# The gate's input and the heads' norms of a three-head decoder layer, made one projection ahead

## The chip, the cores and the metric

The kernel runs on one core of a Trainium2 chip. The metric is the time of one execution in microseconds (us) on that core, smaller is better. The engines are PE (TensorE, matmuls and transposes, with its weight loads as PEld), DVE (VectorE), ACT (ScalarE), POOL (GpSimd) and SP (SyncE, which here only issues DMAs).

## What is computed

One layer of a decoder on x of 1 x 2048 x 1024 in float32: a norm, one input projection whose columns feed three groups of heads, their outputs through one output projection, then a gated MLP and a last norm. The change touches two of the groups, HGRN2 (A, 4 heads) and gated linear attention (C, 4 heads), cut here to what matters:

```python
def hgrn2_mixer(q, f_logit, i, g, lower_bound, norm_w):
    z = f_logit.astype(jnp.float32)
    f = lb + (1.0 - lb) * jax.nn.sigmoid(z)
    log_f = jnp.log(jnp.maximum(f, F_FLOOR))
    key = (1.0 - lb) * jax.nn.sigmoid(-z)
    o = chunked_gated_linear_attention(heads(q, A_DK), heads(key, A_DK), heads(i, A_DV), heads(log_f, A_DK))
    return head_rmsnorm(o, norm_w) * jax.nn.silu(g)

def gla_mixer(q, k, v, g, g_lr, w_g_up, b_g, norm_w):
    log_f = jax.nn.log_sigmoid((g_lr @ w_g_up + b_g).astype(jnp.float32)) / C_GATE_NORM
    ...
    o = chunked_gated_linear_attention(qh, kh, vh, log_f.reshape(b_sz, t, C_HEADS, C_DK))
    return head_rmsnorm(o, norm_w) * jax.nn.silu(g)
```

`head_rmsnorm` divides each head's 64 outputs of a token by the root of their mean square. `g_lr` is a projection of only 16 columns, the input of the low-rank gate.

## The kernel before

The sequence is worked in four blocks of 512 tokens (`TB`), numbered 0 to 3. For each block there are the projection steps (`in_steps`) and the mixing steps (`mix_steps`). A float32 matmul is made of three, on a high and a low part of each operand (`mm3`), so a projection to 128 columns is 24 matmuls, and each weight tile is first split by two engines into `wh` and `wl` (L106, L108, L113).

The projection steps of a block are: two for z (L252), four for V with the 16 gate columns beside it (L267), the gate (`s_gate`, L276), four for Q and K (`s_qk`, "qk projections") and four more for V. The gate transposes the 16 columns into a PSUM bank (L281), copies them to the tile `lr` (L282), multiplies by the gate's weights (L284) and works out the log decays L on ACT and DVE (L288 to L310). Its tiles come from rings: `lr` from tag X with two buffers, `e` and `u1` from tag t2 with three, the PSUM banks from tag aux with two.

The mixing steps of a block are first 14 level steps and two for the diagonal (`s_level`, `s_diag`): seven levels of 1 to 64 tokens for each half of the block. A level makes exponentials of L in a tile of tag X (L390, L393 on ACT), the scaled operands qa and kp on DVE (L394, L400) and qc on POOL (four products, L404), and score matmuls (L413, L427). Then come the windows, which apply scores and state, and the mean squares of the outputs O (`s_sq`). The norms of a block's heads (`s_out`) are left in `run["out"]` and are made within the gate of the block after next in program order, that is in the middle of `s_gate` (L303): the roots on ACT (L506, L507), their split into `hl` (L511), the spreading over the heads by 16 matmuls (L516), the product with O (L518) and a store. So block 0's norms are made at the gate of block 2 and block 1's at the gate of block 3. For the last two blocks there is no gate left; block 2's norms stand among the levels of block 3 (L704), block 3's behind its windows (L708).

`run_steps` and `merged` interleave the level steps of one block with the projection steps of the next and the scaling of x for the one after. The steps set the priorities; a scheduler then sets each engine's order, engine by engine, when the program is built. `load_w` lifts the priority of the weights' split by the numbers in `W_SPLIT`.

Of the kernel before, what the change touches and what calls it, by code (L numbers as in the profile page):

```python
# [8 lines left out]
F32 = mybir.dt.float32  # L9
# [7 lines left out]
P = 128  # L17
D = 1024
KT = D // P
TB = 512  # L20
# [24 lines left out]
def kernel(ctx: ExitStack, tc: tile.TileContext, x, norm_mix, w_in, hgrn_lower_bounds, hgrn_norm,  # L45
# [183 lines left out]
    with ExitStack() as cx:  # L229
# [13 lines left out]
        def in_steps(b, B):  # L243
# [29 lines left out]

            def s_gate():  # L276
                V, K, L = B["V"], B["K"], B["L"]
                lr = tmp.tile([16, TB], F32, name="lr", tag="X")
                pt = aux_bank()
                for t in range(NTK):  # L280
                    pe.transpose(out=pt[:16, t * P:(t + 1) * P], in_=V[:, t, 512:528], identity=ident)  # L281
                vec.tensor_copy(lr, pt[:16, :])  # L282
                gl = aux_bank()
                pe.matmul(gl, gup, lr, start=True, stop=True)  # L284
                e, u1 = t2(), t2()
                f = tmp.tile([P, 2, TB], F32, name="f", tag="f", bufs=1)
                z, l01, mn = K[:, 0:2, :], L[:, 0:2, :], L[:, 2, :]
                act.activation(e, gl, AF.Abs, bias=pc["bg"])  # L288
                act.activation(e, e, AF.Exp, scale=-1.0)
                act.activation(f, z, AF.Sigmoid)  # L290
                act.activation(z, z, AF.Sigmoid, scale=-1.0)
                vec.tensor_scalar(mn, gl, pc["bg"], 0.0, op0=ALU.add, op1=ALU.min)
                vec.tensor_scalar(u1, e, 1.0, None, op0=ALU.add)
                vec.scalar_tensor_tensor(e, u1, -1.0, e, op0=ALU.add, op1=ALU.subtract)
                for c in range(2):
                    vec.tensor_scalar(f[:, c, :], f[:, c, :], lb1[:, c:c + 1], lb[:, c:c + 1],
                                      op0=ALU.mult, op1=ALU.add)
                vec.tensor_scalar(l01, f, LN_MIN, None, op0=ALU.max)
                vec.tensor_scalar(f, f, F_FLOOR, LN_MIN, op0=ALU.max, op1=ALU.min)
                act.activation(u1, u1, AF.Ln)  # L300
                act.activation(l01, l01, AF.Ln)
                act.activation(f, f, AF.Ln, scale=LN_UP)
                if run.get("out"):  # L303
                    run.pop("out")()
                vec.tensor_tensor(e, e, u1, op=ALU.subtract)
                vec.tensor_tensor(mn, mn, e, op=ALU.add)
                vec.tensor_scalar(mn, mn, 1.0 / 16.0, None, op0=ALU.mult)
                vec.scalar_tensor_tensor(l01, f, lnc, l01, op0=ALU.subtract, op1=ALU.add)
                for c in range(2):
                    vec.tensor_scalar(K[:, c, :], K[:, c, :], lb1[:, c:c + 1], None, op0=ALU.mult)  # L310
            for t in range(NTK):
                steps.append(lambda t=t: (s_vw(C_V, 272) if t == 0 and b > 0 else None, s_v(272, 256, t)))
            steps.append(s_gate)


            def s_qk(nm, c, col, scale):
                if nm not in B:
# [2 lines left out]
            for nm, c, col, scale in (("Q", 0, A_Q, 1.0), ("Q", 1, A_Q + P, 1.0), ("Q", 2, C_Q, C_SCALE),  # L320
                                      ("K", 2, C_K, 1.0)):
                steps.append(lambda a=(nm, c, col, scale): s_qk(*a))
            for t in range(NTK):
                steps.append(lambda t=t: (s_vw(A_I, 256) if t == 0 else None, s_v(256, 0, t)))

# [21 lines left out]
        def mix_steps(b, B):  # L347
# [153 lines left out]
                    pe.matmul(ms[32 * c:32 * c + 32, :HT], hcol[:, 0:32], sq[:, c, :], start=True, stop=True)  # L501
                copy(vec, B["ms"][:, sl], ms[:, :HT])

            def s_out():
                O, ms = B["O"], B["ms"]
                act.activation(ms, ms, AF.Ln, bias=eps_t, scale=1.0 / 64.0)  # L506
                act.activation(ms, ms, AF.Exp, scale=-0.5)  # L507
                for hb in range(NH):
                    sl = slice(hb * HT, (hb + 1) * HT)
                    hl = tmp.tile([P, 2, HT], F32R, name="hl", tag="t2", bufs=3)  # L510
                    split(ms[:, sl], hl[:, 0, :], hl[:, 1, :])  # L511
                    for g2 in range(2):
                        r = aux_bank().rearrange("p (c t) -> p c t", c=2)
                        for c in range(2):
                            for i in range(2):
                                pe.matmul(r[:, c, :], sel[:, 2 * g2 + c, :], hl[:, i, :], start=(i == 0), stop=(i == 1))  # L516
                        cs = slice(2 * g2, 2 * g2 + 2)
                        vec.tensor_tensor(O[:, cs, sl], O[:, cs, sl], r, op=ALU.mult)  # L518
# [6 lines left out]
            for hb in range(NH):  # L525
                steps2.append(lambda hb=hb: s_decay(hb))
                steps2 += [lambda hb=hb, w=w: s_window(hb, w) for w in range(NW)]
                steps2.append(lambda hb=hb: s_sq(hb))
            steps2.append(lambda: run.update(out=s_out))
            return steps, steps2  # L530


# [158 lines left out]
            blocks[b]["hT"] = norms[b].hT  # L691
            return steps

        ins = ins[0:2] + ins[3:5] + ins[2:3] + ins[5:]
        run_steps(ins, prep(1), 0.5, 0.7)
        for b in range(NB):
            lv, wn = mix_steps(b, blocks[b])
# [3 lines left out]
                lv = lv[3:]  # L701
            if b == NB - 1:
                lv_prio = tc.cur_priority
                mid = [run.pop("out")] if NB > 1 else []  # L704
                run_steps(lv, bg + mid, 0.0, 0.6)
                ac_prio = tc.cur_priority
                run_steps(wn)
                run.pop("out")()  # L708
            else:
                ins, late, bg = in_steps(b + 1, blocks[b + 1])  # L710
                run_steps(lv, merged(ins, prep(b + 2)), 0.0, 0.6)
# [603 lines left out]
```

## Time and profile before

| | us |
|---|---|
| median of 3 runs | 2220.92 |
| lowest and highest | 2212.77, 2224.83 |
| the profiled execution | 2215.95 |
| its span on the core | 2214.2 |
| PE busy in the span | 2142.7 (97%) |
| DVE busy | 1678.8 (76%) |
| ACT busy | 987.5 (45%) |
| POOL busy | 349.3 (16%) |

The profile is of one execution. Its page gives each engine's busy time, and the trace behind it can be asked for stretches of the span, for what an engine waited for and what ended the wait, and for the instructions of an engine in order of time. Matmuls are pipelined and their ends are modelled, so a matmul of 512 columns is shown longer than the distance to the next one. The mixer of the A and C groups, in which the changed code lies, takes about the first 640 us of the span; behind it come the B group, the output projection and the MLP, whose code is the same before and after.

### The profile page before, as it was taken

What the parts mean: (1) busy time and instruction counts of PE and PEld (TensorE: products, weight loads), DVE (VectorE), ACT (ScalarE), POOL (GpSimd) and SP (SyncE); (2) the same over time, 40 slices, a digit from 0 to 9 for tenths busy, and PEclk for the clock granted to TensorE, in tenths of its full rate; (3) what the DMA queues carried; (4) which work ended last, traced back from release to release, by engine and by line L of the source; (5) the groups of instructions that cost most, each with busy time, mean ns of one, the idle gap of its engine ahead of it and who ended that gap; (6) DMA issues with size and microseconds to landing.
All of it is one profiled execution on the core that took longest, in us unless ns stands there. A gap on an engine that the chain in (4) does not pass through costs nothing.

```text
span 2214.2 us, 31440 instructions
## 1 busy us (share of the span) xinstructions
PE 2142.7 (97%) x12118; PEld 1761.8 (80%) x12118; DVE 1678.8 (76%) x2366; ACT 987.5 (45%) x1361; POOL 349.3 (16%) x456
## 2 busy tenths in 40 slices
PE   7999999999899999999999999999999999999998
PEld 6887778777667878988888887788888887888886
DVE  7799998988768778786676766666666678679676
ACT  3453535433156467454444445544444455226332
POOL 2232341516333231000000000000000000000000
PEclk9999999999999999999999999999999999999999
DMA  7352432345144736643342435522222258667653
GB/s 260 116 180 73 162 97 65 96 148 184 60 136 176 225 121 190 202 136 119 110 134 87 133 95 182 190 80 86 86 86 86 85 176 276 209 205 254 217 174 111
DMA packets 313699, 321.41 MB, mean 145 GB/s; under 512 B 17347, under 2 KB 267214, under 8 KB 312014
## 3 DMA queue, kind: packets, MB, share of 16 engines
q1 hardware_dynamic: 313550, 319.41, 44.5%
q8 instruction: 95, 1.56, 0.3%
q14 instruction: 54, 0.44, 0.1%
HBM read 233.38 MB, written 85.98 MB: 144 GB/s over the span
## 4 chain that ended last, share of the span: by engine, by line
PE 54%; DVE 7%; DMA 5%; ACT 2%; issue 2%; POOL 0%; SPq 0%; DVEq 0%; POOLq 0%; ACTq 0%
PE mm L1072 26%; PE sc L1072 13%; PE aux L1072 6%; PE sc L137 2%; PE sc L138 2%; PE sc L136 2%; DVE wl L113 1%; DMA x_d<-xr 1%; PE mm L138 1%; PE mm L136 1%; PE mm L137 1%; DMA xt<-x_d 1%; DVE xc L801 1%; DMA y<-ps_d 1%; PE mm L913 1%
## 5 line engine op out<-in xcount | busy, mean ns | idle before, releaser
L106 ACT ACTIVATE wh<-wr 128x1024 fp32r<-128x1024 f32 (+3 forms) x217 | 200.8, 928 | 354.6 <-PE mm L1072 91.2
L113 DVE TENSOR_TENSOR wl<-wr,wh 128x1024 fp32r<-128x1024 f32 (+2 forms) x241 | 260.8, 1085 | 102.5 <-ACT wh L106 98.3
L106 ACT ACTIVATE wh<-s 128x1024 fp32r<-128x1024 f32 x116 | 123.0, 1062 | 251.7 <-PE sc L1072 197.8
L138 PE MATMUL mm<-hTh,wl 128*128 128x512 f32 x576 | 231.0, 401 | 2.8 <-POOL wl L113 2.4
L136 PE MATMUL mm<-hTh,wh 128*128 128x512 f32 x576 | 233.6, 406 | 0.0
L137 PE MATMUL mm<-hTl,wh 128*128 128x512 f32 x576 | 231.7, 402 | 0.0
L404 POOL TENSOR_TENSOR qc<-Q,X 32x128 f32<-32x128 f32 x224 | 151.0, 674 | 247.3 <-ACT X L390 116.4
L1072 PE MATMUL mm<-t34h,wh 128*128 128x512 f32 x464 | 181.1, 390 | 1.3 <-DVE y L1238 0.9
L1072 PE MATMUL mm<-t34h,wl 128*128 128x512 f32 x464 | 180.6, 389 | 0.0
L1072 PE MATMUL mm<-t34l,wh 128*128 128x512 f32 x464 | 180.5, 389 | 0.0
L113 DVE TENSOR_TENSOR wl<-s,wh 128x1024 fp32r<-128x1024 f32 x116 | 141.4, 1221 | 18.5 <-ACT wh L106 18.4
L137 PE MATMUL sc<-wl,oh 128*128 128x256 f32 x512 | 146.8, 287 | 2.4 <-DVE wl L113 2.4
L136 PE MATMUL sc<-wh,oh 128*128 128x256 f32 x512 | 146.3, 287 | 0.2 <-DVE xr L834 0.2
L138 PE MATMUL sc<-wh,ol 128*128 128x256 f32 x512 | 145.4, 284 | 0.0
L138 PEld LDWEIGHTS mm<-hTh,wl 128*128 128x128 f32 x576 | 108.6, 189 | 31.1 <-issue 4.3
L136 PEld LDWEIGHTS mm<-hTh,wh 128*128 128x128 f32 x576 | 108.4, 188 | 28.9 <-issue 6.8
L137 PEld LDWEIGHTS mm<-hTl,wh 128*128 128x128 f32 x576 | 108.7, 189 | 27.8 <-issue 7.3
L1141 DVE SCALAR_TENSOR_TENSOR ga<-gr,pcol,ga 128x1024 f32<-128x1024 f32 x84 | 107.6, 1281 | 0.4 <-issue 0.3
L1072 PEld LDWEIGHTS mm<-t34h,wh 128*128 128x128 f32 x464 | 87.1, 188 | 21.2 <-issue 1.7
L137 PEld LDWEIGHTS sc<-wl,oh 128*128 128x128 f32 x512 | 97.5, 190 | 5.8 <-DVE wl L113 3.0
L1072 PEld LDWEIGHTS mm<-t34h,wl 128*128 128x128 f32 x464 | 87.1, 188 | 18.2
L1072 PEld LDWEIGHTS mm<-t34l,wh 128*128 128x128 f32 x464 | 87.1, 188 | 17.9
(335 smaller groups left out, 5508.4 us busy)
## 6 DMA issues: line engine op xcount, KB each, us to landing
wr<-in_w_in_dram SPq DMA_DIRECT2D x80, 512.0 KB
wr<-in_ffn_w_gate_dram SPq DMA_DIRECT2D x42, 512.0 KB
wr<-in_ffn_w_val_dram SPq DMA_DIRECT2D x42, 512.0 KB
wr<-in_w_out_dram SPq DMA_DIRECT2D x32, 512.0 KB
gr_d<-v SPq DMA_DIRECT2D x32, 512.0 KB
ps_d<-y SPq DMA_DIRECT2D x32, 512.0 KB
wr<-gr_d SPq DMA_DIRECT2D x32, 512.0 KB
wr<-in_ffn_w_down_dram SPq DMA_DIRECT2D x25, 512.0 KB
```

Source lines behind the costliest of these rows:

```text
L106: act.activation(o, i, AF.Copy)
L113: e_lo.tensor_tensor(lo, raw, hi.bitcast(F32), op=ALU.subtract)
L136: pe.matmul(o, lh, rh, start=first, stop=False)
L137: pe.matmul(o, lh, rl, start=False, stop=False)
L138: pe.matmul(o, ll, rh, start=False, stop=last)
L404: pool.tensor_tensor(qc[p_, h, :].rearrange("p (n s) -> p n s", s=lev), qo[p_, 2], xo[p_, 2], op=ALU.mult)
L801: vec.tensor_tensor_scan(xc[:, i, :], r[:, i, :], th[:, i, :], initial=hs0[:, c:c + 1], op0=ALU.mult, op1=ALU.add)
L913: pe.transpose(out=pt[:, k * P:(k + 1) * P], in_=xt[:, (k0 + k) * P:(k0 + k + 1) * P], identity=ident)
L1072: pe.matmul(o, lhs[a], rhs[b], start=first and k == 0 and i == 0, stop=last and k == KH - 1 and i == 2, skip_group_check=True)
L1141: vec.scalar_tensor_tensor(ga, gr[:, k:k + TH], pc[f"fw{k}"][:, f:f + 1], ga, op0=ALU.mult, op1=ALU.add)
```

## The change

The gate is cut in two steps. `s_gate_in` transposes and copies `lr` and calls the first part of the norms, if there are any; `s_gate` multiplies, calls the second part of the norms at once (before its own work on ACT and DVE), and goes on as before. In the list of steps `s_gate_in` stands behind the first qk projection and `s_gate` behind the second; before, the whole gate stood ahead of the first one (in block 0 behind the second, by a line that is now gone). `s_out` is cut in the same way: `s_out_in` makes the roots and both `hl`, `s_out` the matmuls, the products and the store. Where block 2's norms stand among the levels, the two parts are now two steps; at the end they follow each other.

```diff
--- before.py
+++ after.py
@@ -273,15 +273,21 @@
 
 
 
-            def s_gate():
-                V, K, L = B["V"], B["K"], B["L"]
-                lr = tmp.tile([16, TB], F32, name="lr", tag="X")
+            def s_gate_in():
+                lr = B["lr"] = tmp.tile([16, TB], F32, name="lr", tag="X")
                 pt = aux_bank()
                 for t in range(NTK):
-                    pe.transpose(out=pt[:16, t * P:(t + 1) * P], in_=V[:, t, 512:528], identity=ident)
+                    pe.transpose(out=pt[:16, t * P:(t + 1) * P], in_=B["V"][:, t, 512:528], identity=ident)
                 vec.tensor_copy(lr, pt[:16, :])
+                if run.get("out"):
+                    run["out"][0]()
+
+            def s_gate():
+                K, L = B["K"], B["L"]
                 gl = aux_bank()
-                pe.matmul(gl, gup, lr, start=True, stop=True)
+                pe.matmul(gl, gup, B["lr"], start=True, stop=True)
+                if run.get("out"):
+                    run.pop("out")[1]()
                 e, u1 = t2(), t2()
                 f = tmp.tile([P, 2, TB], F32, name="f", tag="f", bufs=1)
                 z, l01, mn = K[:, 0:2, :], L[:, 0:2, :], L[:, 2, :]
@@ -300,8 +306,6 @@
                 act.activation(u1, u1, AF.Ln)
                 act.activation(l01, l01, AF.Ln)
                 act.activation(f, f, AF.Ln, scale=LN_UP)
-                if run.get("out"):
-                    run.pop("out")()
                 vec.tensor_tensor(e, e, u1, op=ALU.subtract)
                 vec.tensor_tensor(mn, mn, e, op=ALU.add)
                 vec.tensor_scalar(mn, mn, 1.0 / 16.0, None, op0=ALU.mult)
@@ -310,8 +314,6 @@
                     vec.tensor_scalar(K[:, c, :], K[:, c, :], lb1[:, c:c + 1], None, op0=ALU.mult)
             for t in range(NTK):
                 steps.append(lambda t=t: (s_vw(C_V, 272) if t == 0 and b > 0 else None, s_v(272, 256, t)))
-            steps.append(s_gate)
-
 
             def s_qk(nm, c, col, scale):
                 if nm not in B:
@@ -320,6 +322,9 @@
             for nm, c, col, scale in (("Q", 0, A_Q, 1.0), ("Q", 1, A_Q + P, 1.0), ("Q", 2, C_Q, C_SCALE),
                                       ("K", 2, C_K, 1.0)):
                 steps.append(lambda a=(nm, c, col, scale): s_qk(*a))
+
+            steps.insert(NTK + 3, s_gate_in)
+            steps.insert(NTK + 5, s_gate)
             for t in range(NTK):
                 steps.append(lambda t=t: (s_vw(A_I, 256) if t == 0 else None, s_v(256, 0, t)))
 
@@ -501,14 +506,21 @@
                     pe.matmul(ms[32 * c:32 * c + 32, :HT], hcol[:, 0:32], sq[:, c, :], start=True, stop=True)
                 copy(vec, B["ms"][:, sl], ms[:, :HT])
 
-            def s_out():
-                O, ms = B["O"], B["ms"]
+            def s_out_in():
+                ms = B["ms"]
                 act.activation(ms, ms, AF.Ln, bias=eps_t, scale=1.0 / 64.0)
                 act.activation(ms, ms, AF.Exp, scale=-0.5)
+                B["hl"] = []
+                for hb in range(NH):
+                    hl = tmp.tile([P, 2, HT], F32R, name="hl", tag="t2", bufs=3)
+                    split(ms[:, hb * HT:(hb + 1) * HT], hl[:, 0, :], hl[:, 1, :])
+                    B["hl"].append(hl)
+
+            def s_out():
+                O = B["O"]
                 for hb in range(NH):
                     sl = slice(hb * HT, (hb + 1) * HT)
-                    hl = tmp.tile([P, 2, HT], F32R, name="hl", tag="t2", bufs=3)
-                    split(ms[:, sl], hl[:, 0, :], hl[:, 1, :])
+                    hl = B["hl"][hb]
                     for g2 in range(2):
                         r = aux_bank().rearrange("p (c t) -> p c t", c=2)
                         for c in range(2):
@@ -526,7 +538,7 @@
                 steps2.append(lambda hb=hb: s_decay(hb))
                 steps2 += [lambda hb=hb, w=w: s_window(hb, w) for w in range(NW)]
                 steps2.append(lambda hb=hb: s_sq(hb))
-            steps2.append(lambda: run.update(out=s_out))
+            steps2.append(lambda: run.update(out=(s_out_in, s_out)))
             return steps, steps2
 
 
@@ -691,7 +703,6 @@
             blocks[b]["hT"] = norms[b].hT
             return steps
 
-        ins = ins[0:2] + ins[3:5] + ins[2:3] + ins[5:]
         run_steps(ins, prep(1), 0.5, 0.7)
         for b in range(NB):
             lv, wn = mix_steps(b, blocks[b])
@@ -701,11 +712,12 @@
                 lv = lv[3:]
             if b == NB - 1:
                 lv_prio = tc.cur_priority
-                mid = [run.pop("out")] if NB > 1 else []
+                mid = list(run.pop("out")) if NB > 1 else []
                 run_steps(lv, bg + mid, 0.0, 0.6)
                 ac_prio = tc.cur_priority
                 run_steps(wn)
-                run.pop("out")()
+                for f in run.pop("out"):
+                    f()
             else:
                 ins, late, bg = in_steps(b + 1, blocks[b + 1])
                 run_steps(lv, merged(ins, prep(b + 2)), 0.0, 0.6)
```

PE, around the gate of block 2 (at about 260 us). The rows in a row before; `mm` is a projection, `aux<-ident,V` the transposes for the gate, `aux<-lr,gup` the gate's matmul:

```order
L281 MATMUL aux<-ident,V 16x128 x4
L136 MATMUL mm<-hTh,wh 128x512
L137 MATMUL mm<-hTl,wh 128x512
L138 MATMUL mm<-hTh,wl 128x512
L136 MATMUL mm<-hTh,wh 128x512
L137 MATMUL mm<-hTl,wh 128x512
L138 MATMUL mm<-hTh,wl 128x512
L136 MATMUL mm<-hTh,wh 128x512
L137 MATMUL mm<-hTl,wh 128x512
L138 MATMUL mm<-hTh,wl 128x512
L136 MATMUL mm<-hTh,wh 128x512
L284 MATMUL aux<-lr,gup 128x512
```

And now, at the end of the second qk projection, where the gate's matmul and the norms' matmuls (`aux<-hl,sel`) come:

```order
L137 MATMUL mm<-hTl,wh 128x512
L138 MATMUL mm<-hTh,wl 128x512
L288 MATMUL aux<-lr,gup 128x512
L528 MATMUL aux<-hl,sel 128x256 x4
L432 MATMUL sc<-qa_549,kp_547 64x64 x4
L432 MATMUL sc<-qc_551,kp_547 64x128 x2
L432 MATMUL sc<-qa_549,kp_547 64x64 x4
L432 MATMUL sc<-qc_551,kp_547 64x128 x2
L136 MATMUL mm<-hTh,wh 128x512
L137 MATMUL mm<-hTl,wh 128x512
L528 MATMUL aux<-hl,sel 128x256 x4
```

The transposes have moved a projection ahead of the gate's matmul, the gate's matmul a projection and a half later, and the norms' matmuls, which stood within the first two projections, stand directly behind it, with a level's score matmuls (`sc`) next.

DVE, around the gate of block 3 (at about 390 us), before: the subtraction that makes the low part of `hl` stands within the gate's work (L292, L293, L294):

```order
L108 CAST wh<-wr 128x1024
L292 TENSOR_SCALAR L<-aux,pcol_412 128x512
L293 TENSOR_SCALAR t_4083<-t_4082 128x512
L400 TENSOR_TENSOR qa_550<-Q,X 64x2x128
L294 SCALAR_TENSOR_TENSOR t_4082<-t_4083,t_4082 128x512
L113 TENSOR_TENSOR hl<-ms,hl 128x256
L113 TENSOR_TENSOR wl<-wr,wh 128x1024
L518 TENSOR_TENSOR O<-O,aux 128x2x256 x2
L113 TENSOR_TENSOR hl<-ms,hl 128x256
```

And now, at the start of block 3's projections, where K is copied from the z projections:

```order
L361 TENSOR_TENSOR pr<-Q,K 128x768
L377 COPY_PREDICATED sd_543<-mdiag,dsb 128x1024
L113 TENSOR_TENSOR hl<-ms,hl 128x256
L108 COPY K<-mm 128x512
L113 TENSOR_TENSOR wl<-wr,wh 128x816
L113 TENSOR_TENSOR hl<-ms,hl 128x256
L108 COPY K<-mm 128x512
L108 COPY dT<-aux 96x256
L113 TENSOR_TENSOR wl<-wr,wh 128x544
```

Both subtractions have moved ahead by some 30 instructions, to the copies of K from the two z projections.

ACT, around the gate of block 2, before; X is a level's tile, L290 and L291 are the sigmoids and L301 and L302 the logarithms of the gate:

```order
L290 ACT_TABLE_LOAD
L290 ACTIVATE f<-K 128x1024
L291 ACTIVATE K<-K 128x1024
L301 ACT_TABLE_LOAD
L301 ACTIVATE L<-L 128x1024
L302 ACTIVATE f<-f 128x1024
L390 ACT_TABLE_LOAD
L390 ACTIVATE X<-L 128x192x2
L393 ACTIVATE X<-X 128x192x2
```

And now:

```order
L395 ACTIVATE X<-L 128x384
L395 ACTIVATE X<-L 128x192x2
L297 ACT_TABLE_LOAD
L297 ACTIVATE K<-K 128x1024
L398 ACT_TABLE_LOAD
L398 ACTIVATE X<-X 128x192x2
L307 ACT_TABLE_LOAD
L307 ACTIVATE L<-L 128x1024
L308 ACTIVATE f<-f 128x1024
L321 ACTIVATE Q<-mm 128x512
L395 ACT_TABLE_LOAD
L395 ACTIVATE X<-L 128x192x2
```

The two sigmoids no longer stand together, so that exponentials come between them with a table load each way (two more loads stand just ahead of these rows), and the last exponential of X here comes behind the copy of Q out of the first qk projection.

## Rows read from the trace of the kernel before

**Rows 1.** Stretches: from:to, length, busy PE, PEld, DVE, ACT, POOL, clock, DMA, GB/s
```profile
246.00:321.00 75.00, 69.14 (x614) 57.55 (x615) 72.25 (x118) 35.56 (x54) 34.73 (x51) 1.00 0.29 85
321.00:376.00 55.00, 54.78 (x469) 42.84 (x469) 47.11 (x88) 21.06 (x34) 2.97 (x4) 1.00 0.28 78
376.00:449.00 73.00, 69.02 (x602) 57.09 (x603) 69.55 (x115) 35.21 (x52) 35.42 (x52) 1.00 0.25 74
...
540.00:571.00 31.00, 23.94 (x195) 18.27 (x192) 30.59 (x45) 5.32 (x11) 18.91 (x27) 1.00 0.57 203
```

**Rows 2.** PE's waits, 120 to 571 us: releaser, us in total, times, longest
```profile
PE sc L427 <- DVE qa L400: 9.4, 8, 2.8
PE sc L413 <- DVE qa L400: 4.1, 5, 1.9
PE aux L516 <- DVE hl L113: 2.2, 3, 1.2
...
PE aux L281 <- DVE V L108: 1.3, 2, 1.1
...
PE aux L284 <- DVE lr L282: 0.4, 2, 0.3
PE aux L516 <- DVE O L518: 0.4, 1, 0.4
```

**Rows 3.** PE in order of time: start, us, instruction, idle before and releaser
```profile
269.99 0.97 PE L516 MATMUL aux<-hl,sel 128*128 128x256 f32 x6 [0.73 <-DVE hl L113]
...
274.68 0.39 PE L136 MATMUL mm<-hTh,wh 128*128 128x512 f32 x1
274.91 0.39 PE L137 MATMUL mm<-hTl,wh 128*128 128x512 f32 x1
...
541.34 0.98 PE L516 MATMUL aux<-hl,sel 128*128 128x256 f32 x6 [1.17 <-DVE hl L113]
...
558.72 0.42 PE L427 MATMUL sc<-qa,kp 128*32 128x64 f32 x8 [2.79 <-DVE qa L400]
```

**Rows 4.** DVE in order of time, pauses and the subtractions of hl
```profile
247.44 0.44 DVE L108 COPY V<-mm 128x272 f32<-128x272 f32 x1 [0.51 <-PE mm L138]
...
257.10 0.69 DVE L108 CAST wh<-wr 128x1024 fp32r<-128x1024 f32 x1 [0.37 <-PE mm L138]
...
371.34 0.69 DVE L108 COPY K<-mm 128x512 f32<-128x512 f32 x1 [2.69 <-PE mm L138]
...
397.57 0.68 DVE L113 TENSOR_TENSOR hl<-ms,hl 128x256 fp32r<-128x256 f32 x1
...
400.50 0.41 DVE L113 TENSOR_TENSOR hl<-ms,hl 128x256 fp32r<-128x256 f32 x1
```

**Rows 5.** ACT in order of time, around the gate at 260 us
```profile
245.53 1.28 ACT L290 ACT_TABLE_LOAD   x1
246.82 1.06 ACT L290 ACTIVATE f<-K 128x1024 f32<-128x1024 f32 x1
...
265.19 0.52 ACT L390 ACTIVATE X<-L 128x384 f32<-128x384 f32 x1
...
272.62 0.58 ACT L319 ACTIVATE Q<-mm 128x512 f32<-128x512 f32 x1
```

**Rows 6.** POOL in order of time, the four products of one level
```profile
256.73 3.82 POOL L404 TENSOR_TENSOR qc<-Q,X 32x128 f32<-32x128 f32 x4 [5.28 <-ACT X L390]
```

**Rows 7.** DVE in order of time, lr and the level behind it
```profile
260.45 1.21 DVE L113 TENSOR_TENSOR wl<-wr,wh 128x1024 fp32r<-128x1024 f32 x1
...
262.68 0.71 DVE L282 COPY lr<-aux 16x512 f32<-16x512 f32 x1
263.32 0.53 DVE L392 TENSOR_TENSOR X<-L 128x384 f32<-128x384 f32 x1
263.78 0.54 DVE L397 TENSOR_TENSOR L<-L 128x384 f32<-128x384 f32 x1
264.25 0.41 DVE L400 TENSOR_TENSOR qa<-Q,X 64x256 f32<-64x256 f32 x1
```

## The prediction

> **What bounds the kernel now.** The page's table of engines comes first: PE is busy 97% of the span, so little can be won outside its waits, and the question is whether the waits that the edit aims at set the end. I read three views for that, in this order. The first gives each engine's busy time by stretches of the mixer stage [rows 1]. The reader is to see two kinds of stretch taking turns. From 246 to 321 us, where block 2's projections run beside the levels of block 1, DVE works 72.25 of 75 us and PE 69.14; the same pair for block 3 (376 to 449 us) has DVE at 69.55 of 73; the levels of the last block (540 to 571 us) have DVE at 30.59 of 31 and PE at 23.94. Between them, in the windows from 321 to 376 us, PE works 54.78 of 55 and DVE has slack. So around both gates that also hold the norms, DVE is the bound and PE is the engine that waits; DVE's idle time there, 2.75 + 3.45 + 0.41 = 6.6 us, is all that a better order can take out of these stretches without taking work out of DVE.
>
> The second view is what PE waited for between 120 and 571 us [rows 2]. The three kinds of matmul that the edit touches wait 1.3 us (transposes for V, two waits), 0.4 us (the gate's matmul for lr, two) and 2.2 + 0.4 us (the norms' matmuls for hl and for O, four): 4.3 us in eight waits. The levels' score matmuls wait far more, 9.4 + 4.1 us, and always for DVE. The third is PE's order of time [rows 3]: the norms' matmuls stand 0.73 us at 269.99 and 1.17 us at 541.34, but after the last of these the levels' matmuls wait 2.79 us at 558.72 before the same stretch is over. A PE that is let go earlier at the first place waits longer at the second, as long as DVE's work ends when it ended.
>
> **The change part by part.** *No work is added but table loads.* The same matmuls, copies and subtractions are issued.
>
> *The waits of transposes, gate and norms.* They sum to 4.3 us of idle time [rows 2]. The idle time is counted from the modelled end of the matmul before, 0.39 us after its start, while the next one could have started 0.23 us after it [rows 3], so each of the eight hides up to 0.16 us more: 4.3 + 8 x 0.16 = 5.6 us at most. In the new order the norms' matmuls stand directly behind the gate's and their hl is made a whole projection ahead, so these PE waits go. What is late next is DVE's queue in the same stretch: the score matmuls of the last levels. I therefore count 0 of the 5.6 in the sum and keep 5.6 for the range.
>
> *The subtractions that make hl.* In the block with the gate at 376 to 449 us they took 0.68 + 0.41 us inside the stretch in which DVE is the bound. Now they stand between the copies of the two z projections, where DVE idled 2.69 us for PE at 371.34 [rows 4]. That is work leaving the bound engine's stretch: -1.1 us. For the block before it, with its gate at 246 to 321 us, I take nothing: the same move puts hl there ahead of work of DVE's own, so it is done earlier and not beside a wait.
>
> *Two pauses of DVE on the projections.* At 247.44 and 257.10 DVE waited 0.51 and 0.37 us for PE [rows 4]. With one level step less among the first V tiles PE gets there earlier, so they go: -0.9 us.
>
> *The gate's place.* For blocks 1 to 3 its rest moves behind the second of the qk projections, and with it the levels shift against the projections. The piece of ACT's order shows what this brings: the exp of the next level's X now stands behind the copy of Q out of the first projection and behind a table load, where it stood ahead of them. From the end of that projection to that exp's end it is 0.58 (copy of Q) + 1.28 (load) + 0.52 (exp) = 2.4 us [rows 5], and POOL's four products then take 3.82 us [rows 6]: the scores can start 6.2 us after the projection's end. PE reaches them after 13 matmuls of 0.23 = 3.0 us, so a new PE wait of about 3 us stands in the next projection, once at each of the two gates. What it costs is read on DVE. After the projection's end DVE has the cast of the next weights (0.69, [rows 4]), lr (0.71) and the subtraction (0.53) = 1.9 us before it needs the exp at 2.4: 0.5 idle. Then sum (0.54), two qa (0.41 each), kp (of the sum's shape, 0.54 too) and the weights' low part (1.21) [rows 7] bring it to 5.5; the next level's X has to wait till 6.2, because lr holds one of the two X buffers and POOL reads the other: 0.7 idle; and the copy of the scores waits for PE after that, about 0.4. Together 1.6 us, less about half a microsecond by which I take DVE to come late to that point anyway, with its queue full: +1.1 us at each of two gates, +2.2. Bounds: 0 if DVE is later by 1.6 than I take it, and +5.8 if the whole PE wait of 2 x 2.9 is lost.
>
> *Table loads.* ACT's order has three more of them in the block at 246 us, none more elsewhere: 3 x 1.28 = 3.8 us of ACT [rows 5], which is busy 35.56 of 75 us there [rows 1]. I count 0; the cover is ACT's idle half, and if it is gone, they cost up to 3.8. By the Trainium skill (ScalarE: Activation LUTs, What ACT_TABLE_LOAD costs) a switch of table costs a drain of about 1.38 us beside the load, 2.66 us in all; the rows speak against that here, since the next activation starts 1.29 us after the load began (245.53 and 246.82), and by that page the three would take 8.0 us of ACT and the exp behind each gate would come 1.4 us later.
>
> *The DMA queue.* The store of O moves behind three more weight loads on SP. What it stores is read only after the mixer stage, and O is next written in the windows behind the levels; 0.
>
> *The two places without a projection between.* In the last block the norms' input and matmuls are a level step apart, and at the end of the stage nothing lies between them; PE's order at the end is the old one, so the waits there stay. 0.
>
> The sum: -1.1 - 0.9 + 2.2 = +0.2 us against the profiled execution's 2215.95, 2216.2. The median of the runs shown is 4.97 us above that execution, so the forecast is 2221 us.
>
> **The rivals.** *The gain is kept.* If DVE's queue runs dry less often because PE delivers projections earlier, all of PE's eight waits go and stay gone: -5.6 - 1.1 - 0.9 = -7.6 us, some 2213 us by the median. For it: these waits lie on PE, which is busy 97%. Against it: DVE at 72.25 of 75, and score waits of 13.5 us that can take all of it back [rows 1, 2]. Only more than this, half of those score waits too, would be faster by over 0.5%.
>
> *The wait changes its place and grows (slower).* lr now lives across a projection in a ring of two X buffers. Each level's exps then wait for POOL's four products of the level before, for two levels in a row at each gate; the second costs what POOL is late against DVE's queue, up to one more 3.82 less its own 13 matmuls, about 1 us, and the whole PE wait of 5.8 counts, with the three table loads in front of exps: 5.8 + 2 x 1 + 3.8 - 1.1 = +10.5 us, 2231 us. The point from which it decides: POOL's products against 3.1 us of DVE work that stands behind the exp [rows 6, 7]; at 3.82 POOL is past it by 0.7. For it: the order puts exp behind the copy of Q at both gates. Against it: DVE's own backlog, which makes the same instructions late without any wait.
>
> *It doesn't do what it says.* The scheduler could have put hl and lr where they were. The order shows hl ahead by some 30 DVE instructions at two of its four places and hardly moved at the other two, so this holds in part, and is in the sum.
>
> **How the numbers follow.** Forecast (the waits are traded, +0.2, between -3 and +4): 0.55. Gain kept (-7.6): 0.2. Slower rival (+10.5): 0.25. The measurement tells about 0.5%, 11 us, from no change. The runs of one kernel lie 12 us apart, so a median can be off by 3 or 4: of the gain's 0.2 about 0.1 ends beyond -11, of the slower rival's 0.25 about 0.12 beyond +11, and I add 0.02 on either side for orders that I have not followed. So faster 0.12, same 0.74, slower 0.14. The range reaches to both rivals and leaves out what lies beyond them: 2210 to 2232.
>
> **What would show each step.** Right: the matmuls of gate and norms wait for nothing at the gates of blocks 2 and 3; hl's subtractions stand before 375 us at 0.41 each; the score matmuls inside the second qk projection wait some 3 us for POOL or DVE; DVE stays near 72 of 75. The gain kept would show in the levels' score waits, still 13.5 us or less, and the stretches from 246 and 376 us shorter by 2 to 3 us each. The slower rival would show as DVE idle for POOL in front of the X subtraction, over 1.5 us at each gate. The forecast is wrong if the stretch up to 246 us, or the one before 120 us, in which only the order of projections and x loads changes, moves by more than a microsecond, since I gave both nothing.

## The result, and the profile after

The changed kernel is slower: 2234.59 us median (2229.68 to 2245.16, 8 runs) against 2220.07 for the kernel before (8 runs), a ratio of 1.0079 with a 95% interval of 1.006 to 1.0098, 14.5 us. A second set of runs gave 1.0075 (1.0052 to 1.0098). The prediction said 2221 us, between 2210 and 2232, and gave "slower by over 0.5%" a chance of 0.14: it was wrong.

The profiled execution took 2240.93 us, 25.0 more than that of before. The loss is read first where the levels of blocks 0, 1 and 2 run, beside which the gates of blocks 1, 2 and 3 stand. Each line goes from a block's first diagonal step to its last level-32 score matmul; the columns are those of [rows 1]. The first fence is the kernel before, the second the changed one, blocks 0 to 3 in both:

```profile
72.50:184.80 112.30, 109.43 (x844) 92.28 (x843) 94.80 (x151) 47.44 (x74) 36.56 (x56) 1.00 0.45 142
212.20:314.80 102.60, 96.00 (x855) 79.23 (x853) 95.81 (x161) 49.01 (x78) 39.17 (x54) 1.00 0.43 145
346.60:443.20 96.60, 92.82 (x839) 76.74 (x837) 87.25 (x150) 48.61 (x72) 36.00 (x52) 1.00 0.28 80
477.10:559.60 82.50, 77.67 (x626) 59.70 (x625) 72.37 (x107) 28.89 (x51) 44.41 (x56) 1.00 0.61 205
sum 394.00, PE 375.93 PEld 307.96 DVE 350.23 ACT 173.95 POOL 156.15; mean PE 93.98 PEld 76.99 DVE 87.56 ACT 43.49 POOL 39.04
```

```profile
75.80:193.70 117.90, 110.18 (x827) 92.86 (x827) 96.25 (x153) 47.61 (x75) 38.76 (x56) 0.98 0.43 135
222.60:329.70 107.10, 98.16 (x854) 81.55 (x854) 94.51 (x162) 53.34 (x81) 34.52 (x55) 0.98 0.41 139
361.40:461.00 99.60, 93.31 (x838) 77.59 (x836) 87.12 (x150) 48.27 (x72) 32.56 (x52) 0.98 0.27 77
494.90:577.30 82.40, 77.37 (x626) 59.69 (x624) 72.38 (x106) 28.89 (x51) 44.43 (x56) 1.00 0.61 205
sum 407.00, PE 379.02 PEld 311.68 DVE 350.25 ACT 178.12 POOL 150.27; mean PE 94.75 PEld 77.92 DVE 87.56 ACT 44.53 POOL 37.57
```

DVE's work is the same to 0.02 us (350.23 and 350.25), and the stages are 13.0 us longer: all of that is new idle time of DVE, 4.15 us beside the gate of block 1, 5.80 beside that of block 2, 3.13 beside that of block 3, nothing in the block without a gate. The mean clock of the three stages fell from 1.00 to 0.98, so a part of this idle time may be DVE waiting for a slower PE. Of the other 12 us of the profiled difference 5.6 lie between 605 and 656 us, where the clock is lower (below), and some 3.3 ahead of the first stage; of these 1.46 are left at 107 us. Read between the same matmuls (106.43, 183.94, 312.47 and 442.30 us before; 107.89, 192.24, 326.88 and 460.12 us now), the stretches of the three gates take 6.8, 6.1 and 3.4 us longer.

What PE waited for from 120 to 590 us in the changed kernel, the view of [rows 2]:

```profile
PE sc L432 <- DVE qa L405: 15.8, 11, 3.2
PE sc L432 <- POOL qc L409: 3.4, 3, 1.3
PE mm L136 <- DVE wh L108: 2.6, 2, 1.4
PE sc L418 <- DVE qa L405: 2.1, 2, 1.7
...
PE aux L528 <- DVE hl L113: 1.5, 1, 1.5
```

The transposes and the gate's matmul wait no more, the norms' matmuls only once (in the last block). But the score matmuls wait 15.8 + 2.1 us for DVE where they waited 13.5, and 3.4 us for POOL, where it was 0.2.

The place where it begins, at the gate of block 2: ACT, POOL, DVE and PE of the changed kernel in order of time, as in [rows 5], [rows 6], [rows 7] and [rows 3].

```profile
276.38 0.60 ACT L321 ACTIVATE Q<-mm 128x512 f32<-128x512 f32 x1 [8.70 <-PE mm L138]
277.00 1.28 ACT L395 ACT_TABLE_LOAD   x1
278.29 0.56 ACT L395 ACTIVATE X<-L 128x384 f32<-128x384 f32 x1
```

```profile
257.59 5.73 POOL L409 TENSOR_TENSOR qc<-Q,X 32x128 f32<-32x128 f32 x8 [1.12 <-ACT X L395]
...
278.93 4.12 POOL L409 TENSOR_TENSOR qc<-Q,X 32x128 f32<-32x128 f32 x4 [15.61 <-ACT X L395]
```

```profile
278.88 0.56 DVE L402 TENSOR_TENSOR L<-L 128x384 f32<-128x384 f32 x1 [0.97 <-ACT X L395]
...
283.08 0.56 DVE L397 TENSOR_TENSOR X<-L 128x384 f32<-128x384 f32 x1 [0.41 <-POOL qc L409]
284.21 1.30 DVE L441 COPY_PREDICATED sd<-mask,sc 128x512 f32<-128x512 int32 x1 [0.58 <-PE sc L432]
```

```profile
281.36 0.45 PE L432 MATMUL sc<-qa,kp 128*64 128x64 f32 x8 [1.72 <-DVE qa L405]
283.10 0.44 PE L432 MATMUL sc<-qc,kp 128*64 128x128 f32 x4 [1.28 <-POOL qc L409]
```

ACT stands idle for 8.70 us in front of the copy of Q, because its instructions run in their order and that copy needs the projection's end; the next level's exponential is queued behind the copy and a table load. POOL had finished the level before at 263.3 and stands idle 15.61 us. When the exponential is through, DVE, POOL and PE wait in turn. The same waits come at the gate of block 3 (PE 1.71 and 1.28 at 415 and 417 us) and smaller ones at that of block 1 (PE 0.36 and 0.82 at 153 and 155, DVE 1.40 us for POOL at 155).

### The profile page after: what moved, and what is told of

It reads as the page before. It is cut to its first block, busy times and chain, and to the rows that moved or that the text cites. A ratio compares the mean times of both kernels' runs of the same rounds, so it can differ in the third digit from the quotient of the medians.

```text
span 2239.2 us, 31437 instructions
## 1 busy us (share of the span) xinstructions
PE 2155.9 (96%) x12118; PEld 1772.6 (79%) x12118; DVE 1677.6 (75%) x2366; ACT 992.8 (44%) x1364; POOL 347.4 (16%) x456
## 4 chain that ended last, share of the span: by engine, by line
PE 53%; DVE 6%; DMA 5%; ACT 3%; issue 2%; POOL 0%; SPq 0%; DVEq 0%; POOLq 0%; ACTq 0%
PE mm L1084 26%; PE sc L1084 13%; PE aux L1084 6%; DMA x_d<-xr 1%; PE sc L137 1%; PE sc L138 1%; PE sc L136 1%; DMA xt<-x_d 1%; DVE wl L113 1%; DMA y<-ps_d 1%; PE mm L136 1%; PE mm L138 1%; PE mm L137 1%; DVE xc L813 1%; PE mm L925 1%
## 5 line engine op out<-in xcount | busy, mean ns | idle before, releaser
L409 POOL TENSOR_TENSOR qc<-Q,X 32x128 f32<-32x128 f32 x224 | 144.4, 645 | 279.7 <-ACT X L395 175.7
```

Source lines behind the costliest of these rows:

```text
L409: pool.tensor_tensor(qc[p_, h, :].rearrange("p (n s) -> p n s", s=lev), qo[p_, 2], xo[p_, 2], op=ALU.mult)
```

## The experiments

Ratios are to runs of the kernel before on the same chip, with their 95% intervals. The edits are cut to what matters (`...`); they are against the changed kernel, or, where the text says so, against the kernel before.

**The two halves of the change.** The gate alone (cut and moved; the norms whole, as before):

```diff
-                if run.get("out"):
-                    run["out"][0]()
...
-                if run.get("out"):
-                    run.pop("out")[1]()
...
+                if run.get("out"):
+                    run.pop("out")()
```

> The gate is split and moved as in the changed kernel; the norms stay whole, in the middle of the gate. Theory of the order (the next level's exp stands behind the copy of Q on ACT, so POOL's products and then the scores come late, PE waits, and the clock falls after such waits): slower as the changed kernel, 2228 to 2237 us, with score waits of 1 to 2 us for DVE and 1 us for POOL inside the second qk projection at three gates. Theory of the norms (two hl held over a projection take two of three t2 buffers): no slower than before, 2216 to 2224 us.

Measured: 2233.04 us, ratio 1.0078 (1.0047 to 1.0108), with the waits of the changed kernel (1.70 and 1.28 us at 277 and 279 us, 2.94 at 191 us), as the theory of the order expected.

The norms alone (the gate whole at its old place, the norms' first part one V projection ahead):

```diff
+            if b > 1:
+                steps.insert(len(steps) - 1, s_norm_in)
             steps.append(s_gate)
```

> The gate is whole and at its old place; only the norms are in two parts, the first one V projection ahead of the gate. Theory of the order: the exp stands ahead of the copy of Q as before, so 2216 to 2225 us, clock 0.993 or more. Theory of the norms: 2228 us or more.

Measured: 2221.58 us, 1.0022 (1.0004 to 1.004), in the expected range; the mean clock, 0.992 over its runs, is a little below the 0.993 expected. So nearly all of the loss comes with the gate.

**Another place for the same cut.** Both parts of the gate one projection earlier, the input right behind V:

```diff
-            steps.insert(NTK + 3, s_gate_in)
-            steps.insert(NTK + 5, s_gate)
+            steps.insert(NTK + 2, s_gate_in)
+            steps.insert(NTK + 4, s_gate)
```

> Both parts of the change, but the gate's input directly behind V and its matmul behind the first qk projection, so the input is one projection ahead and nothing of the gate is more than one projection later. Theory of the order: ACT has the level's exp ahead of the first copy of Q again, so 2214 to 2224 us. If being split, not the order on ACT, is what costs: 2228 us or more.

Measured: 2223.75 us, 1.0021 (1.0006 to 1.0035), at the end of the expected range, and no score matmul waits for POOL. Here too lr is written one projection before its matmul. So being one projection ahead is not by itself what costs; this place is.

The kernel before with its gate whole, moved behind the second qk projection:

```diff
-            steps.append(s_gate)
...
+            steps.insert(NTK + 4, s_gate)
...
-        ins = ins[0:2] + ins[3:5] + ins[2:3] + ins[5:]
```

> The kernel before with its whole gate moved behind the second qk projection in every block; lr is used at once and no buffer is held over a projection. Theory of the order: the exp stands behind two copies of Q, so slower, 2228 to 2240 us. Theory that lr's hold on one of two X buffers is what costs: 2216 to 2224 us.

Measured: 2229.07 us, 1.0055 (1.0033 to 1.0077), with score waits of 1.60, 1.28 and 2.46 us at 164, 172 and 193 us. The later place is slow for a whole gate too, in which lr is used at once and holds no buffer over a projection.

**Which gate.** The changed kernel with block 1's gate at its old place, and the mirror, blocks 2 and 3 at the old place:

```diff
-            steps.insert(NTK + 3, s_gate_in)
-            steps.insert(NTK + 5, s_gate)
+            steps.insert(NTK + (2 if b == 1 else 3), s_gate_in)
+            steps.insert(NTK + (3 if b == 1 else 5), s_gate)
```

> The changed kernel, but block 1's gate (the one beside the levels of block 0, 130 to 200 us) has both parts at the old place, right behind the projections of V; the gates of blocks 2 and 3 and the norms stay as changed. Theory of three gates: the offset of the changed kernel against the kernel before grew from 1.5 to 8.3 us between 107 and 192 us, so this run gets some 5 to 7 us back: 2227 to 2230 us. Rival, the prediction's own count (block 1's gate costs nothing, all is at blocks 2 and 3): 2233 to 2236 us.

> The mirror of the run with block 1's gate at the old place: here block 1's gate (and block 0's, which has no levels beside it) has the new place, and the gates of blocks 2 and 3 have both parts right behind V. Theory of three gates: the norms-only run was 1.0022 times the kernel before, and block 1's gate adds 5 to 7 us: 2226 to 2230 us, with PE's waits of 0.8 us or more at 154 and near 3 us at 190 us and none for POOL behind 200 us. Rival, the prediction's count (block 1 costs nothing): 2220 to 2223 us.

Measured: 2230.56 us, 1.0047 (1.0031 to 1.0063), and 2230.80 us, 1.0054 (1.0035 to 1.0073). Both times lie within 1 us above the range of the theory of three gates; the mirror has the waits expected (0.82 us at 152, 2.92 at 189, none for POOL behind 200), and beside them new ones of 2.50 and 2.51 us at 283 and 415. Block 1's gate costs about 0.3% either way (0.79 - 0.47, and 0.54 - 0.22 of the norms alone), some 7 us, as many as the 6.8 read between the same matmuls above. The other two together cost about 0.25%, by differences whose intervals are about 0.2% wide on either side: three gates, where the prediction had counted two.

**The held buffer.** In the changed kernel lr is written one projection before its matmul, and takes one of two X buffers for so long. Here it takes one of t2's three instead, and in the second run a part of L that the gate itself writes just behind that matmul, which costs no buffer of any ring:

```diff
-                lr = B["lr"] = tmp.tile([16, TB], F32, name="lr", tag="X")
+                lr = B["lr"] = tmp.tile([16, TB], F32, name="lr", tag="t2", bufs=3)
```

```diff
-                lr = B["lr"] = tmp.tile([16, TB], F32, name="lr", tag="X")
+                lr = B["lr"] = B["L"][:16, 2, :]
```

> The changed kernel with one thing else: the gate's input lr (16 partitions) takes a buffer of the ring t2 and not one of the two buffers X that the levels' exponentials write. The order of ScalarE then has the exponentials of the next level ahead of the copy of Q at the gates of blocks 2 and 3 again, at the price of six more table loads in the program. Theory of the order (the next level's exponential stands behind the copy of Q and a table load because its buffer X is held): PE's waits at the scores of these two gates, 1.72 + 1.28 and 1.71 + 1.28 us in the changed kernel, fall under 1 us each, and the time falls from 2235 to some 2222 to 2229 us. Rival, the place (the gate's VectorE work now falls on other levels, whatever buffer lr has): the waits stay or go to the next level, and the time stays at 2231 to 2238 us.

> The changed kernel, but lr stands in 16 partitions of the third part of L, which the gate itself writes right behind its matmul: no buffer X and none of t2. Theory of the held buffer (lr, written one projection before its matmul, holds one of the two X buffers and keeps the next level's exponential behind the copy of Q): at least the 6 us at equal clock that lr in t2 gave back are given back, without the cost of t2's ring: 2218 to 2225 us, no wait of the scores for POOL and none near 3 us at the level-32 scores of block 0. Rival, the place (the gate behind the second projection of Q costs whatever buffer lr has, as with the whole gate there, which stayed at 2241 us with lr in t2): 2226 to 2234 us.

Measured: 2223.62 us, 1.0035 (1.0012 to 1.0057), and 2225.74 us, 1.0022 (1.0006 to 1.0037). The second run's stages, and ACT at the gate of block 2:

```profile
74.30:188.30 114.00, 109.57 (x829) 92.13 (x828) 95.11 (x151) 50.13 (x76) 39.99 (x56) 0.99 0.45 140
215.70:319.20 103.50, 97.42 (x855) 80.86 (x853) 94.50 (x161) 55.94 (x83) 36.56 (x54) 0.98 0.44 143
351.10:449.00 97.90, 93.52 (x839) 77.68 (x837) 87.26 (x150) 51.17 (x74) 31.61 (x52) 0.98 0.27 79
```

```profile
266.75 0.52 ACT L395 ACTIVATE X<-L 128x384 f32<-128x384 f32 x1
...
271.39 0.58 ACT L321 ACTIVATE Q<-mm 128x512 f32<-128x512 f32 x1
```

The exponential now stands ahead of the copy of Q, the waits for POOL and the 2.94 us at block 0's level-32 scores are gone, and the three stages take 9.2 us less than in the changed kernel (324.6 became 315.4; before 311.5). So its data can be ready before the copy's; in the changed kernel it stood behind the copy, and ACT idle. The first run is in the range of its theory; the second is between those of theory and rival. ACT's order has nine table loads more than before here, three more in the changed kernel: the number of loads does not decide the time.

Is the buffer all of it? The same gate with lr in L, but the norms whole, beside the changed kernel on one chip:

> The gate cut in two and moved as in the changed kernel, the norms whole as before, and lr in the third part of L. Theory that the shares add up (norms' split 0.22%, gate's move 0.57%, all of the latter from lr in the ring X): no difference from the kernel before, ratio 0.998 to 1.003, 2215 to 2226 us. Rival (the place itself costs beside the buffer, and the norms' split then happens to cost nothing in the run with lr in L): ratio 1.003 to 1.006, 2226 to 2233 us.

> The changed kernel once more, on the same chip and beside the same runs of before as the run of the gate alone with lr in L. Expected: ratio 1.006 to 1.010 again, 2230 to 2240 us. The theory of the held buffer says the other run of this call lies at least 8 us under it; the rival says at most 5.

Measured: 2227.80 us, 1.0043 (1.0028 to 1.0057), against 2236.80 us, 1.0075. The two differ by 9 us, in the buffer and also in the norms, which are cut in the second alone. Since the gate alone with lr in X lost as much as the whole change (1.0078), the 9 us are put down to the buffer; the like pairs of runs give it 0.35% (gate alone, 1.0078 and 1.0043) and 0.44 or 0.57% (whole change, 1.0079 and 1.0035 or 1.0022). With 0.43% left the shares do not add up, and the rival holds for the rest: the place costs beside the buffer. One row of it is a level-32 score wait of 3.91 us at 321.56 us.

**lr out of the ring elsewhere.** The kernel before with lr in t2 and in L, the gate one projection earlier with both, the whole gate at the later place with both (the line that makes lr is edited as above; the place as in the runs above):

> The kernel before, with lr alone moved from the ring X to the ring t2. Theory of the ring: at the old place too lr takes one of the two X buffers, but gives it back at once, so there is little to gain: 2214 to 2219 us against 2218 to 2219 for the kernel before. Rival (the ring of t2, which the gate's own e and u1 and the norms' hl use, becomes the narrow place, and the exponentials that come earlier bring more table loads): 2220 to 2226 us.

> The kernel before with lr in the third part of L. Theory of the held buffer: before gives X back at once, so only little is held: 2214 to 2219 us. Rival (the exponentials that then run ahead of the gate's logarithms push the gate itself back on ScalarE, which is what cost 5.6 us at equal clock with lr in t2, not t2's ring): 2220 to 2226 us.

> The run with both parts of the gate one projection earlier (gate's input right behind V, gate behind the first projection of Q; 2223.75 us), with lr in the ring t2. Theory of the ring: the exponentials run ahead of the copies of Q at all gates and the 2 us that run kept over the kernel before at equal clock go: 2214 to 2220 us, and if any version of this change beats the kernel before it is this one. Rival (what is left is the norms' split and more table loads): 2221 to 2226 us.

> The run with both parts one projection earlier (2223.75 us; 2228.04 with lr in t2), with lr in the third part of L. Theory of the held buffer: 2215 to 2221 us, the best of all versions. Rival (exponentials ahead of the gate's logarithms push the gate back, PE waits for V's copy as with lr in t2): 2223 to 2229 us.

> The kernel before with its gate whole and moved behind the second projection of Q, as in the place-only run (2229 us), but lr in a buffer of the ring t2 and not in one of the two X. Theory of the ring (what the gate costs at its later place is that lr takes a turn of the two X buffers, so that the next level's exponentials stand behind the copies of Q): 2219 to 2224 us, and PE's waits of the place-only run at 164 and 172 us (1.60 and 1.28) and for POOL at 425 us (0.85) go or fall under half. Rival, the place alone (the gate's work collides with other levels whatever lr's buffer is): 2227 to 2231 us with waits of the same size.

> The kernel before with the whole gate behind the second projection of Q (2229 us; 2241 with lr in t2), and lr in the third part of L. Theory that t2's ring made the 6 us wait for lr's copy at 418 us: 2218 to 2226 us. Rival, the place: 2227 to 2236 us.

Measured, in this order: 1.0008 (0.9985 to 1.003), 1.0014 (0.9997 to 1.003), 1.0038 (1.0022 to 1.0053), 1.0041 (1.0024 to 1.0057), 1.009 (1.0064 to 1.0116), 1.0062 (1.0042 to 1.0083); in us 2222.29, 2220.52, 2228.04, 2227.65, 2241.59 and 2235.53. The theory missed all six: four times lie in the rival's range, and two (2228.04 and 2241.59) above both. Nowhere but with the cut gate at the changed kernel's place does a free X buffer help. The two homes of lr agree within their intervals, so nothing shows that t2's ring is what harms. With the whole gate the wait only moves, here from the run with lr in L:

```profile
417.93 2.04 PE L284 MATMUL aux<-L,gup 16*128 16x512 f32 x2 [5.99 <-DVE L L282]
```

PE stands 6 us because the copy of lr comes late in DVE's order. "lr in the ring is the cause" is therefore shown for the changed kernel alone, and there for a part of its loss. No version was measured faster than the kernel before.

## The granted clock behind the new waits

In its profiled execution the kernel before is at full clock (2.4 GHz) from 0 to 640 us. The changed kernel drops to the lower level (1.2 GHz) for a few microseconds behind most of its longer waits; a stretch in which the column after POOL's is below 1.00 holds such a drop. First the line of before and that of the changed kernel:

```profile
0.00:640.00 640.00, 602.47 (x4656) 476.14 (x4657) 542.82 (x944) 252.98 (x391) 204.79 (x287) 1.00 0.41 130
```

```profile
0.00:640.00 640.00, 595.67 (x4556) 474.24 (x4557) 527.86 (x921) 246.09 (x380) 191.33 (x281) 0.97 0.39 125
```

Then three drops of the changed kernel, first from its first profile, then from its second one, in which the same instructions stand 1 to 3 us earlier:

```profile
192.00:200.00 8.00, 7.76 (x44) 5.26 (x45) 5.56 (x11) 2.05 (x4) 1.79 (x4) 0.60 0.00 0
280.00:292.00 12.00, 9.35 (x71) 6.70 (x72) 9.36 (x14) 4.94 (x9) 5.86 (x10) 0.86 0.18 50
608.00:622.00 14.00, 14.00 (x47) 8.52 (x45) 2.56 (x4) 1.34 (x2) 2.72 (x2) 0.51 0.14 37
```

```profile
190.00:200.00 10.00, 9.10 (x56) 6.55 (x57) 8.74 (x16) 3.11 (x5) 1.80 (x4) 0.83 0.04 11
279.00:291.00 12.00, 10.72 (x74) 7.79 (x70) 7.83 (x12) 4.92 (x9) 4.74 (x9) 0.72 0.22 59
607.00:622.00 15.00, 15.00 (x51) 9.07 (x50) 3.29 (x5) 1.33 (x2) 2.72 (x2) 0.54 0.13 35
```

The first two pairs stand behind the waits of 2.94 us at 192 and of 1.72 + 1.28 us at 281 and 283. Other drops, in both profiles too, stand behind waits of 1.87 us at 129, 3.16 at 327, 1.71 + 1.28 at 415 and 417 and 2.79 at 576. A wait does not always bring one: in the run of the gate alone the same wait of 2.94 us, at 191, is followed by full clock:

```profile
190.00:200.00 10.00, 8.95 (x64) 6.28 (x64) 9.74 (x18) 3.11 (x5) 2.26 (x4) 1.00 0.01 2
```

The last pair has no such wait directly ahead of it (2.79 us at 576, 1.67 at 588), and it costs most: the work between 605.1 and 656.2 us took 45.5 us before (586.5 to 632.0), 51.1 now. It came in both profiles of the changed kernel and in 5 of the 15 other experiments, which share no part of the edit (the norms alone is one, the whole gate with lr in t2 another); why is open. The profile of the gate alone has no drop there, and with 2232.43 us that execution is about as slow as the changed kernel, so this drop is not needed for the loss.

A size for all runs comes from their mean clocks. Within the runs of one kernel, those at a lower mean clock are longer: over 239 runs of the kernels here, each taken about its own kernel's mean, 0.001 of mean clock goes with 1.84 us (0.83 of the 2.22 that it is of the span, standard error 0.03). The changed kernel's 8 runs have a mean clock of 0.9895, the 101 runs of before 0.9932: 0.0037, or 6.8 of the 17.1 us between their means. So by this relation about 10 us are idle time and some 7 go with the clock. Of the 10 us between the mean of all 14 runs of the changed kernel and that of the run with lr in L as its one edit (mean clock 0.9893 and 0.9919), it puts 5 with the clock, and of the 25.0 us between the two profiled executions (0.989 and 0.995) 11: this pair shows more of the clock than the medians do. It is a relation among runs; no experiment held the waits and changed the clock alone.

## Why the prediction was wrong

- **What bounds the kernel: right.** DVE's busy time sets these stretches; it stayed the same, and the three stages grew by what DVE's idle time grew [rows 1].
- **The eight waits, counted 0: right.** Those at the gates went, and the score waits grew instead [rows 2].
- **hl and DVE's pauses, -1.1 and -0.9: the right direction, and too small to matter.** The wait for K in front of which hl now stands fell from 2.69 us [rows 4] to 2.0, and the wait of 0.51 us for V at the gate of block 2 went.
- **The gate's place, +2.2: the step that failed.** Its mechanism was the right one, instruction by instruction: exponential behind the copy of Q and a load, POOL's four products, PE and DVE waiting (predicted 2.9 us of PE wait at a gate, where its own 6.2 and 3.0 us make 3.2; measured 1.72 + 1.28). DVE's pauses right there, worked out as 0.5 + 0.7 + 0.4 = 1.6 us, measured 0.97 + 0.41 + 0.58 = 1.96. Wrong was what followed. First, half a microsecond was taken off at each gate because DVE would be late anyway; no row showed that, and the pauses came in full. Second, only these pauses were counted. In the stage of block 2's gate DVE idled 5.80 us more, since the shifted order made it wait elsewhere too (the fences below): 3.5 us for ACT's part of the weights against 1.2 before, 1.0 more for an exponential, 0.6 for the product with O. Third, it was counted at two gates, and block 1's, to which the forecast gave nothing, costs as much: 4.15 us of DVE idle, about 0.3% in both runs that took it apart. The prediction's own sign for this, a stretch up to 246 us that moves by more than a microsecond, came with 6.8 us. Where +2.2 stood, 13 us of DVE idle time were measured in the profile, a part of them in stretches of lower clock. DVE's waits of the kernel before from 212 to 315 us and of the changed kernel from 222 to 330 us; of the last five lines the kernel before has none:

```profile
DVE wl L113 <- ACT wh L106: 1.2, 2, 0.7
```

```profile
DVE wl L113 <- ACT wh L106: 3.5, 3, 1.3
...
DVE L L402 <- ACT X L395: 1.0, 1, 1.0
DVE kp L399 <- ACT X L398: 1.0, 1, 1.0
DVE sd L441 <- PE sc L432: 0.6, 1, 0.6
...
DVE O L530 <- PE aux L528: 0.6, 1, 0.6
DVE X L397 <- POOL qc L409: 0.4, 1, 0.4
```

- **The clock, not in the sum at all.** A PE wait was priced as if nothing followed it. By the relation above about 7 us go with a lower clock.
- **Table loads, 0: not shown apart.** The run with nine loads more than before is faster than the one with three, but it differs in the buffer too. The load at 277.00 us stands ahead of the exponential for which DVE waits 0.97 us; the prediction had one such load within the gate's place. The exponential began 1.29 us after its load (277.00 and 278.29), and the load 0.02 us after the copy's end (276.38 + 0.60). The Trainium skill (ScalarE: Activation LUTs, What ACT_TABLE_LOAD costs) has a drain of about 1.38 us beside the load; no such drain shows here, nor in [rows 5].
- **Two places without a projection between, 0: right**, 82.50 and 82.40 us in the last block's stage.
- **The start, 0:** a matmul at 106.43 us before stood at 107.89 in the first profile and at 106.56 in the second; the first has a stretch of lower clock at its start (0.97 over the first 60 us, against 1.00). By the second profile the order there costs 0.1 us.
- **The rivals.** The slower one (lr holds one of two X buffers, +10.5) named the cause that the runs then showed for a part of the loss: lr out of that ring gives 0.35 to 0.57% back. It was given 0.25, and weighed down with "DVE's own backlog", for which no row was given but DVE's busy share. That its 2231 us came near is in part luck: its sign, DVE idle for POOL by over 1.5 us in front of the X subtraction at each gate, did not come (0.41 us at the gates of blocks 2 and 3, 1.40 at that of block 1), and it had neither block 1's gate nor the clock.

What stays open: the 0.2 to 0.4% that remain without the held buffer, and why the same wait is followed by a lower clock in one program and not in another: 2.79 us in the last block (574 to 584 us at 0.83 in the changed kernel, 555 to 565 us at 1.00 before), 2.94 us at block 0's level-32 scores (0.60 in the changed kernel, 1.00 with the gate alone).

## What to carry to other kernels

A tile that is written earlier is held longer: before moving its maker, ask which ring its buffer is from and what the next user of that ring will be queued behind, since an engine that works in its order then idles with its data ready. What such a hold costs depends on the place: here the ring gave back 0.35 to 0.57% at one place, and nothing one projection earlier. Price a changed interleaving by the idle time of the bound engine over the whole stage and at every place where the pattern stands, not by the one chain that is easy to follow. And an idle stretch of TensorE can cost more than itself, where a lower clock follows: 8 us at 0.60 behind the wait of 2.94 us.

## What was not expected of the hardware

The drops of TensorE's clock came at the same places of the program in two executions of the changed kernel (the stretches above), so they go with the order of its work and not with chance alone. But the wait ahead of a drop does not settle it: the gate alone, with the same 2.94 us, kept full clock there. The longest drop, 14 us at 0.51, began some 30 us after the last wait of more than 2 us.
